# Held columns of one output remade on 16 engines' partitions and stored from GpSimd's queue

## The chip, the cores and the metric

The kernel runs on one core of one Trainium2 chip. The metric is the device time of one launch in microseconds (us). The profile gives the span from the first to the last instruction of one execution; the device time of that same execution is somewhat longer.

## The reference

For each of 8 x 12 = 96 heads the kernel multiplies a matrix x by the transpose of a matrix y:

```python
# x, y: [8, 12, 512, 64] float32
np.einsum('bhtc,bhsc->bhts', x, y).astype(np.float32)   # [8, 12, 512, 512]
```

It reads 25.17 MB and writes 100.66 MB.

## The kernel before

**Tiling.** Sixteen heads make a group, so there are 6 groups (`NG`). One load brings 128 partitions of 16 KB of x or y for one group (2 MB). A group has two halves, 12 in all (`NH`), and each half gives 4 outputs (`V`), 48 in all. An output `o` is a tile of 128 partitions of 4096 float32 (2 MB): partition p holds row p // 2 of one of two blocks, by p % 2.

**Stages.** `load` issues the loads from SyncE; the first five are issued inside a `tile_critical` section (line 367), the others as buffers come free. `compress` turns a loaded tile into bf16 (ScalarE, VectorE and GpSimd share it), `mix` rearranges x, and `transposes` makes `xT` and `yT` on VectorE. `all_products` is TensorE's loop: for each output, twice four matmuls of 128x512 into one of two PSUM tensors of four banks (`pms`). `result` copies each PSUM tensor into an output buffer (a slot of `pairs`), on ScalarE, for the very last output on VectorE. `store` issues the output's DMA from SyncE; from output 8 on two outputs go out in one DMA of 4 MB.

**Order and synchronisation.** The order of each engine's instructions is written out by hand. `emit` issues an instruction with the semaphore waits that its reads and writes need, as `need` works them out. A DMA signals a semaphore of its slot (`dma0` and so on), a DMA from GpSimd `dmapool`.

**Output 44** (`SHARED`) is stored in pieces, by `shares`. The 64 even partitions go in one DMA of 1 MB from SyncE. The 64 odd ones are divided, for each half b of 32 partitions: GpSimd issues three DMAs (10 rows, 6 rows, 16 rows), of which the first stores only the columns below N - HELD = 1024; SyncE then stores the columns above for 8 of these 10 rows. Two rows for each b, partitions 17 and 19 above 32b, are left without their last 3072 columns: these are the held columns.

**The held columns** are computed a second time at the end. `again` (line 288) runs 20 small matmuls with up to 16 columns of `xT` as weights, so that quarter c of the held columns comes to lie in the four partitions from 4c on, of which two are wanted. `rest` (line 305) copies the 16 partitions to the buffer `xk0` on VectorE and issues two DMAs from SyncE, one for each b, after the store of outputs 46 and 47 in the same queue. They signal `dma2` (`LAST`), as that store does.

**The end.** GpSimd waits for all semaphores but `dmapool` and `dma2`, clears those, and then waits for and clears the two late ones, one after the other (lines 405 to 415).

Of the kernel before, what the change touches and what calls it, by code (L numbers as in the profile page):

```python
# [9 lines left out]
def kernel(  # L10
# [3 lines left out]
    y: bass.AP,  # L14
    out: bass.AP,
):

# [4 lines left out]
    nc = tc.nc  # L24
    B, H, T, C = x.shape
    _, _, S, _ = y.shape
    P = 128
# [5 lines left out]
    V = G // 4  # L33
    K = 8
# [3 lines left out]
    N = K * S  # L38
    SINGLE = 2 * V
    SHARED = V * NH - V  # L40
    LAST = (V * NH - SINGLE - 2) // 2 % 3 * 2
    HELD = 6 * S
    fp32 = mybir.dt.float32
    bf16 = mybir.dt.bfloat16
    u32 = mybir.dt.uint32
# [9 lines left out]
    def buffer(name, width, dtype):  # L55
        return nc.alloc_sbuf_tensor(name, [P, width], dtype)[:, :]
# [4 lines left out]
    xks = [  # L61
        extra[:, :N // 2].bitcast(bf16) if i == 1 else buffer(f"xk{i}", R * C, bf16)
        for i in range(NG - 1)
    ]
# [9 lines left out]
    xTs = [buffer(f"xT{i}", K * D * E, u32) for i in range(2)]  # L74
    yTs = [buffer(f"yT{i}", D * R // 2, u32) for i in range(2)]
    pms = [nc.alloc_psum_tensor(f"pm{i}", [P, 4, S], fp32)[:, :, :] for i in range(2)]
    engines = {"act": nc.scalar, "dve": nc.vector, "pool": nc.gpsimd, "pe": nc.tensor, "sp": nc.sync}
    sems, ticks, snaps, writer, readers = {}, {}, {}, {}, {}
    known, own = {e: {} for e in engines}, {e: {} for e in engines}

    def need(name, points, told=True):

        best = {}
        for p, v in points:
            if known[name].get(p, 0) < v:
                best[p] = max(best.get(p, 0), v)
        for p, v in list(best.items()):
            if any(snaps[q, w].get(p, 0) >= v for q, w in best.items() if q != p):
                del best[p]
        for p, v in best.items():  # L90
            if told:
                engines[name].wait_ge(sems[p], v)  # L92
            known[name][p] = v
            for q, w in snaps[p, v].items():
                known[name][q] = max(known[name].get(q, 0), w)

    def promise(name, reads, writes):

        points = [writer[r] for r in (*reads, *writes) if r in writer]
        points += [v for w in writes for v in readers.get(w, ())]  # L100
        if name == "pool" and name in ticks:
            points.append((name, ticks[name]))
        return points

    def record(name, p, step, reads, writes, queue=False):
        at = (p, ticks.get(p, 0) + step)
        ticks[p] = at[1]
        if not queue:
            own[name][p] = at[1]
        snaps[at] = {**known[name], **own[name], p: at[1]}  # L110
        for r in reads:
            readers.setdefault(r, []).append(at)
        for w in writes:
            writer[w], readers[w] = at, []

    def signal(p):
        if p not in sems:
            sems[p] = nc.alloc_semaphore(p)
        return sems[p]

    def emit(name, make, reads=(), writes=(), dma=None, by=None, step=1):
        need(name, promise(name, reads, writes))
        p = by or name
        if dma is not None:
            p, step = f"dma{dma}", 16
        make().then_inc(signal(p), step)
        record(name, p, step, reads, writes, dma is not None)

    loaded = {}

    places = [0, 1, 2, 3, 4, 0, 1, 2, 3, 4, 1, 3]
    alone = [0, 2, 4, 0, 1, 3, 2, 4]
    heads = [0, 2, 1, 3]
# [3 lines left out]
    def copy(name, dst, src, reads, writes, by=None):  # L137
        emit(
            name,
            lambda: nc.scalar.activation(dst, src, COPY)  # L140
            if name == "act"
            else engines[name].tensor_copy(dst, src),  # L142
            reads,
            writes,
            by=by,
        )

    def both(*ids):
        return [("slot", i, pm) for i in ids for pm in range(2)]

    def place(ap, pattern):
        name = ap.tensor.name
        return mybir.PhysicalAccessPattern(
            ap=pattern, offset=ap.offset, dtype=ap.dtype, memref=name, memsetref=f"{name}_set"
        )

    def transfer(name, dst, src, to=None, of=None):

        to = to or dst.ap
        of = of or [src.ap[0], *[[1, 1]] * (len(to) - len(src.ap)), *src.ap[1:]]  # L160
        return engines[name].add_instruction(  # L161
            mybir.InstDMACopy(
                name=nc.get_next_instruction_name(),
                engine=engines[name].engine,
                ins=[place(src, of)],
                outs=[place(dst, to)],
                mode="Copy",
                cce_op=mybir.AluOpType.bypass,
                queue={"sp": "qSPDynamicHW", "pool": "qPoolDynamic"}[name],
            )  # L170
        )
# [82 lines left out]
    def all_products():  # L254
# [3 lines left out]
        with nc.Fori(1, V * NH + 1, 2 * V, engines=[nc.tensor.engine]) as first:  # L258
            for half in range(2):
                for j, h in enumerate(heads):  # L260
# [3 lines left out]
                    for p in range(2):  # L264
                        nc.tensor.wait_ge(sems[f"free{p}"], first + at)
                        products(half, h, 4 * p).then_inc(signal("pe"), 1)

    def shares(o, s):

        to, mine = ov[o // V, heads[o % V]], slots[s]  # L270
        line, w = to.ap[0][0], N - HELD

        def part(name, p, n, k, lo=0, hi=N):

            dst, src = to[p // 2:p // 2 + n, p % 2, lo:hi], mine[p:p + 2 * n - 1:2, lo:hi]
            emit(
                name, lambda: transfer(name, dst, src, [[line * n // k, k], [line, n // k], [1, hi - lo]]),
                reads=both(s), dma="pool" if name == "pool" else s,
            )

        for b in range(2):
            for p, n, k, hi in ((1, 10, 5, w), (21, 6, 3, N), (65, 16, 8, N)):
                part("pool", 32 * b + p, n, k, 0, hi)
        emit("sp", lambda: transfer("sp", to[:, 0], mine[::2]), reads=both(s), dma=s)
        for b in range(2):
            part("sp", 32 * b + 1, 8, 4, w)

    def again():

        half, h, part = SHARED // V % 2, heads[SHARED % V], HELD // 4  # L290
        xT = xTs[half].bitcast(bf16).rearrange("p (k h m) -> p k h m", k=K, h=V)
        yT = yTs[half].bitcast(bf16)
        for c in range(3, -1, -1):
            begin, end = N - HELD + c * part, N - HELD + (c + 1) * part
            cuts = sorted({begin, end, *range(begin, end, S), *(n for n in range(0, N, S) if begin < n < end)})
            for lo, hi in zip(cuts, cuts[1:]):
                for b in range(2):
                    last = nc.tensor.matmul(  # L298
                        pms[0][:4 * c + 4, 2 * b + (lo - begin) // S, (lo - begin) % S:(lo - begin) % S + hi - lo],
                        xT[:, lo // S, h, 32 * b + 16 - 4 * c:32 * b + 20],  # L300
                        yT[:, h * S + lo % S:h * S + lo % S + hi - lo], start=True, stop=True,
                    )
        return last

    def rest():

        half, part = SHARED // V % 2, HELD // 4
        to = ov[SHARED // V, heads[SHARED % V]]
        mine = xks[0][:16].bitcast(fp32)[:, :2 * part].rearrange("p (b s) -> p b s", b=2)
        emit("pe", again, [("xT", half), ("yT", half)], [("pm", 0)])  # L310
        copy(
            "dve", mine, pms[0][:16].rearrange("p (b j) s -> p b (j s)", b=2)[:, :, :part],
            [("pm", 0)], [("xk", 0)],
        )
        for b in range(2):
            dst, src = to[16 * b + 8:16 * b + 10, 1, N - HELD:], mine[1::2, b]
            emit(
                "sp", lambda: transfer(
                    "sp", dst, src, [[part, 4], dst.ap[0], [1, part]], [src.ap[0], [1, 1], src.ap[-1]]
                ),  # L320
                reads=[("xk", 0)], dma=LAST,
            )

    def store(o):
# [39 lines left out]
            for part in range(4):  # L364
                mix(i + 1, "dve", part)

    with tc.tile_critical():  # L367
        for n in range(SLOTS):
            load(n)
    tc.close()  # L370
# [26 lines left out]
    for o in range(V, V * NH):  # L397
        result(o)
        if o % V == V - 1:
            prepare(o // V + 2)  # L400
    all_products()
    rest()
    emit("sp", nc.sync.nop)

    last = f"dma{LAST}"
    late = ["dmapool", last]
    others = [p for p in sems if p not in late]
    need("pool", [(p, ticks[p]) for p in others])
    numbers = sorted(sems[p].num for p in others)
    runs = [n for n in numbers if n - 1 not in numbers]  # L410
    for n in runs:
        nc.gpsimd.sem_clear(range(n, next(m for m in range(n, n + len(sems) + 1) if m not in numbers)))
    for p in late:
        need("pool", [(p, ticks[p])])
        nc.gpsimd.sem_clear(sems[p])


# [28 lines left out]
```

## Time and profile before

| what | before |
|---|---|
| median of 3 runs | 297.98 us (297.93 to 298.37) |
| the profiled execution | 297.92 us |
| its span | 296.1 us |
| DMA traffic | 125.85 MB, 425 GB/s over the span |
| SyncE's queue | 5888 packets, 125.03 MB |
| GpSimd's queue | 288 packets, 0.80 MB |
| busy share of the span: PE, DVE, ACT, POOL | 47%, 53%, 70%, 20% |
| remade matmuls (line 298) | 20, 3.3 us |
| copy of the held columns on VectorE | 16 partitions x 1536, 1.7 us |
| stores of the held columns | 2 from SyncE, 24 KB each |

In the profile's lines PE is TensorE, DVE VectorE, ACT ScalarE, POOL GpSimd and SP SyncE; a q behind a name means the engine's sequencer. q1 is the DMA queue that SyncE's DMAs go through and q0 the one of GpSimd's. A group is shown as engine, line, operation, output<-input, number, busy time. The DMA row has one digit for each fortieth of the span: the busy share of the 16 DMA engines in tenths.

### The profile page before, as it was taken

The page shows a single profiled execution, that of the slowest core. Times are in us where ns is not written, and L with a number is a line of the kernel's source. Part 1 is how long each engine was busy: PE and PEld are TensorE (multiplying, and loading weights), DVE is VectorE, ACT ScalarE, POOL GpSimd, SP SyncE. Part 2 cuts the span into 40 slices and gives each one's busy share as a digit, 9 for nine tenths or more (in the row PEclk, how much of TensorE's full clock was granted, in tenths as well). Part 3 has the DMA queues.
Part 4 walks back from the last instruction along what each step waited for, and adds up shares of the span by engine and source line. Part 5 has one row for each costly group of instructions (what it writes and reads, how often), then busy time and mean ns, then how long its engine had stood idle before and what let it go on. Part 6 is the DMA issues. An engine that isn't in the chain of part 4 may idle for free.

```text
span 296.1 us, 1231 instructions
## 1 busy us (share of the span) xinstructions
PE 139.9 (47%) x404; PEld 37.9 (13%) x404; DVE 158.0 (53%) x76; ACT 208.2 (70%) x107; POOL 59.5 (20%) x29
## 2 busy tenths in 40 slices
PE   0000040437576557556654655577546646575400
PEld 0000010112111111111111111111111111121200
DVE  2167798899929594925808529258095240002600
ACT  1664666999999999666966696669666976684000
POOL 2399999992000000000000000000000000040000
PEclk9999995657779997778789776765798787756855
DMA  7999999999999999999999999999999999999998
GB/s 272 427 429 427 432 429 427 432 425 425 427 438 427 460 425 426 425 429 447 429 456 426 425 429 425 425 438 434 434 456 425 425 429 429 425 438 422 415 436 348
DMA packets 6178, 125.85 MB, mean 425 GB/s; under 512 B 896, under 2 KB 896, under 8 KB 932
## 3 DMA queue, kind: packets, MB, share of 16 engines
q1 hardware_dynamic: 5888, 125.03, 98.7%
q0 software_dynamic: 288, 0.80, 0.7%
q14 instruction: 2, 0.02, 0.0%
HBM read 25.17 MB, written 100.66 MB: 425 GB/s over the span
## 4 chain that ended last, share of the span: by engine, by line
DMA 56%; ACT 23%; PE 7%; issue 4%; DVE 3%; SPq 0%; ACTq 0%
DMA out_dram<-pair 43%; ACT pair L140 21%; DMA pair<-in_y_dram 7%; DMA pair<-in_x_dram 6%; PE pm L248 6%; DVE pair L142 3%; ACT xk L140 1%; PE pm L298 1%; ACT yb L140 1%; DVE xk L142 1%; SPq L177 0%; ACTq L92 0%; SPq L371 0%; SPq L367 0%
## 5 line engine op out<-in xcount | busy, mean ns | idle before, releaser
L248 PE MATMUL pm<-yT,xT 128*128 128x512 bf16 x384 | 136.6, 501 | 137.3 <-ACT pair L140 100.0
L140 ACT ACTIVATE pair<-pm 128x2048 f32<-128x2048 f32 x94 | 170.6, 1883 | 41.3 <-DMA out_dram<-pair 37.5
L225 DVE STREAM_TRANSPOSE xT<-xb 128x2048 uint32<-128x2048 uint32 x12 | 46.7, 3893 | 69.1 <-PE pm L248 66.7
L248 PEld LDWEIGHTS pm<-yT,xT 128*128 128x128 bf16 x384 | 36.0, 115 | 237.0 <-ACT pair L140 156.0
L161 POOL DMA_DIRECT2D out_dram<-pair x6 | 3.5, 583 | 193.7 <-ACT pair L140 193.7
L142 DVE COPY xb<-xk 32x2048 bf16<-32x2048 bf16 x32 | 41.7, 1304 | 0.9
L142 DVE CAST yb<-pair 64x2048 bf16<-64x2048 f32 x10 | 30.7, 3074 | 9.5 <-DMA pair<-in_y_dram 9.3
L140 ACT ACTIVATE xk<-pair 128x4096 bf16<-128x4096 f32 x5 | 18.1, 3617 | 10.4 <-DMA pair<-in_x_dram 10.3
L142 POOL COPY xb<-xk 32x2048 bf16<-32x2048 bf16 x8 | 23.5, 2939 | 6.7 <-ACT xk L140 6.2
L142 DVE COPY pair<-pm 128x2048 f32<-128x2048 f32 x2 | 4.5, 2286 | 31.9 <-PE pm L248 31.9
L234 DVE STREAM_TRANSPOSE yT<-yb 128x1024 uint32<-128x1024 uint32 x10 | 19.2, 1918 | 0.0
L140 ACT ACTIVATE yb<-pair 64x2048 bf16<-64x2048 f32 x5 | 12.4, 2472 | 3.9 <-DMA pair<-in_y_dram 3.8
L142 POOL CAST yb<-pair 64x2048 bf16<-64x2048 f32 x5 | 14.5, 2903 | 1.2 <-DMA pair<-in_y_dram 0.8
L142 POOL COPY xb<-pair 32x2048 bf16<-32x2048 bf16 x4 | 12.7, 3184 | 0.3
L140 ACT ACTIVATE pair<-pair 128x4096 bf16<-128x4096 f32 (+1 forms) x2 | 6.1, 3030 | 3.7 <-DMA pair<-in_x_dram 2.5
L142 DVE CAST pair<-pair 64x2048 bf16<-64x2048 f32 x2 | 5.4, 2694 | 4.0 <-DMA pair<-in_y_dram 4.0
L142 DVE COPY xb<-pair 32x2048 bf16<-32x2048 bf16 x4 | 5.2, 1306 | 0.1
L140 ACT ACT_TABLE_LOAD x1 | 1.3, 1283 | 4.4 <-PEq L371 4.4
L378 DVE MEMSET xb<- 128x2048 uint32 x1 | 1.8, 1765 | 4.9 <-PEq L371 4.9
L234 DVE STREAM_TRANSPOSE yT<-pair 128x1024 uint32<-128x1024 uint32 x2 | 3.9, 1946 | 0.0
L298 PE MATMUL pm<-yT,xT 128*16 128x256 bf16 (+5 forms) x20 | 3.3, 333 | 0.6 <-DVE pair L142 0.6
L142 POOL CAST pair<-pair 64x2048 bf16<-64x2048 f32 x1 | 3.3, 3293 | 0.1
(7 smaller groups left out, 5.8 us busy)
## 6 DMA issues: line engine op xcount, KB each, us to landing
out_dram<-pair SPq DMA_DIRECT2D x19, 4096.0 KB, 21.8
out_dram<-pair SPq DMA_DIRECT2D x9, 2048.0 KB, 9.3
pair<-in_x_dram SPq DMA_DIRECT2D x6, 2048.0 KB, 18.8
pair<-in_y_dram SPq DMA_DIRECT2D x6, 2048.0 KB, 16.5
out_dram<-pair SPq DMA_DIRECT2D x1, 1024.0 KB
out_dram<-pair POOLq DMA_DIRECT2D x2, 256.0 KB, 16.6
out_dram<-pair SPq DMA_DIRECT2D x2, 96.0 KB
out_dram<-pair POOLq DMA_DIRECT2D x2, 96.0 KB, 14.6
```

What stands on the lines that cost most here:

```text
L140: lambda: nc.scalar.activation(dst, src, COPY)
L142: else engines[name].tensor_copy(dst, src),
L161: return engines[name].add_instruction(mybir.InstDMACopy(name=nc.get_next_instruction_name(), engine=engines[name].engine, ins=[place(src, ...
L225: lambda: nc.vector.transpose(xTs[half].rearrange("p (k r e) -> p k e r", k=K, e=E), xbs[half].rearrange("p (k e c) -> p k e c", k=K, e=E),),
L234: lambda: nc.vector.transpose(yTs[half].rearrange("p (r j) -> p j r", r=D), ybs[half][b].rearrange("p (j c) -> p j c", c=D),),
L248: last = nc.tensor.matmul(pms[k // 4][:, j, :], xT[:, k + j, h, :], yT[:, h * S:(h + 1) * S], start=True, stop=True,)
L298: last = nc.tensor.matmul(pms[0][:4 * c + 4, 2 * b + (lo - begin) // S, (lo - begin) % S:(lo - begin) % S + hi - lo], xT[:, lo // S, h, 32 ...
L378: lambda: engines[name].memset(xbs[half], 0.0),
```

## The change

- 7 instead of 6 blocks of 512 columns are held (`HELD`), so 3584 columns. GpSimd's first DMA of each b stores 512 columns of its ten rows, and SyncE's DMAs 3584 columns of eight rows.
- `again` cuts the held columns into eighths of 448 columns. Eighth q of half b is remade in the partitions from 64b + 4q on. To place it there, the weights begin 64b + 4q columns of `xT` ahead of the wanted ones; what lies below is written over by the pieces that come later in the loop. There are 28 matmuls, all into one PSUM bank.
- `rest` copies 96 partitions of 448 columns on VectorE, and GpSimd instead of SyncE issues the stores: three DMAs, of 5, 3 and 8 eighths (`turns`), with two rows of 448 columns in each. They signal `dmapool`.
- `shares` takes its division of the odd rows from the same `turns`; rows and engines are as before.
- The semaphores of `late` are allocated first, so that each set of semaphores is one range: GpSimd waits for the early ones and clears them at once, then waits for both late ones and clears them at once.
- The section with the first five loads is synchronised by ScalarE in place of SyncE, whose loads it holds.

```diff
-    HELD = 6 * S
+    HELD = 7 * S
...
+    turns = [(0, 5), (5, 3), (8, 8)]
...
+    late = [f"dma{LAST}", "dmapool"]
+    for p in late:
+        signal(p)
...
+    def part(name, dst, src, k, reads, dma):
+        assert src.ap[0][1] == 2 * k and dst.ap[0][1] == k
+        emit(
+            name, lambda: transfer(name, dst, src, dst.ap),
+            reads=reads, dma=dma,
+        )
...
     def shares(o, s):
...
+        def odd(name, b, e, k, lo, hi):
+            p = 4 * e + 32 * b + (32 if e > 7 else 0)
+            n = 2 * k
+            dst = to[p // 2:p // 2 + n, 1, lo:hi].rearrange("(k i) n -> k i n", i=2)
+            part(name, dst, mine[p + 1:p + 2 * n:2, lo:hi], k, both(s), "pool" if name == "pool" else s)
         for b in range(2):
-            for p, n, k, hi in ((1, 10, 5, w), (21, 6, 3, N), (65, 16, 8, N)):
-                part("pool", 32 * b + p, n, k, 0, hi)
+            for e, k in turns:
+                odd("pool", b, e, k, 0, N if e else w)
         emit("sp", lambda: transfer("sp", to[:, 0], mine[::2]), reads=both(s), dma=s)
         for b in range(2):
-            part("sp", 32 * b + 1, 8, 4, w)
+            odd("sp", b, 0, 4, w, N)
...
     def again():
...
+        for b in (1, 0):
+            for q in range(7, -1, -1):
+                begin, end = N - HELD + q * width, N - HELD + (q + 1) * width
+                cuts = [begin, *(n for n in range(0, N, S) if begin < n < end), end]
+                for lo, hi in zip(cuts, cuts[1:]):
+                    stop = (lo // S * V + h) * P + 32 * b + 20
                     last = nc.tensor.matmul(
+                        pms[0][:64 * b + 4 * q + 4, 0, lo - begin:hi - begin],
+                        xT[:, stop - 64 * b - 4 * q - 4:stop],
...
     def rest():
...
+        mine = xks[0][:64 + 32].bitcast(fp32)[:, :width]
         emit("pe", again, [("xT", half), ("yT", half)], [("pm", 0)])
+        copy("dve", mine, pms[0][:64 + 32, 0, :width], [("pm", 0)], [("xk", 0)])
+        for e, k in turns:
+            b, q = divmod(e, 8)
+            dst = to[16 * b + 8:16 * b + 10, 1, N - HELD + q * width:N - HELD + (q + k) * width]
+            p = 64 * b + 4 * q
+            part(
+                "pool", dst.rearrange("i (k n) -> k i n", n=width), mine[p + 1:p + 4 * k:2],
+                k, [("xk", 0)], "pool",
             )
...
-    with tc.tile_critical():
+    with tc.tile_critical(sync_engine=nc.scalar.engine):
...
+    for points in ([p for p in sems if p not in late], late):
+        need("pool", [(p, ticks[p]) for p in points])
+        numbers = [sems[p].num for p in points]
+        assert max(numbers) - min(numbers) == len(points) - 1
+        nc.gpsimd.sem_clear(range(min(numbers), max(numbers) + 1))
```

## The prediction

> **What bounds the kernel now.** I read the page's slices and queue table first, then the packets of the last microseconds, because the change touches only the first microsecond and the last thirty.
>
> The page, span, slices and DMA queues (packets, MB, share of 16 engines):
>
> ```profile
> span 296.1 us, 1231 instructions
> ...
> DMA  7999999999999999999999999999999999999998
> ...
> q1 hardware_dynamic: 5888, 125.03, 98.7%
> q0 software_dynamic: 288, 0.80, 0.7%
> ```
>
> The 16 DMA engines are busy in every slice. In the trace's packet records (start, time, size, queue of each) the first packets start at 1.99 to 2.46 us, and from there the packets of one engine follow each other without a gap. So the end is the first start plus the longest engine's own sum of packet times; work of PE, DVE, ACT or POOL counts only if a store is issued too late, or if it makes packets slower. The question is which engine ends last, and by how much.
>
> The DMA view of 295 to 295.7 us:
>
> ```profile
> DMA packets 34, 0.05 MB, mean 70 GB/s; under 512 B 18, under 2 KB 18, under 8 KB 34
> ...
> q1 hardware_dynamic: 34, 0.05, 18.7%
> ```
>
> These are the held columns: 16 packets of 3072 B (the two stores of `rest`, 24 KB each) and small 4 B completion writes. They take 0.121 us each and run on only four engines, four in a row on each, behind the last 32 KB packets of the store of outputs 46 and 47. By the packet records the 16 engines end their last 32 KB packet between 294.62 and 295.33 us, the four at 295.01, 295.06, 295.17 and 295.20; these four go on to 295.49 to 295.68. The last completion lands 0.34 us later, at 296.02; GpSimd's last semaphore clear ends the span at 296.09. The profiled execution took 297.92 us, so 1.83 us lie outside the span; it stands 0.06 us below the median, 297.98.
>
> How the held columns come about, in the chain of waits (start, us, what), and SyncE's and GpSimd's timelines:
>
> ```profile
> 272.21 2.30 DVE pair L142
> 274.51 0.04 issue
> 274.56 3.35 PE pm L298 x20
> 277.91 0.02 issue
> 277.93 1.75 DVE xk L142
> ```
>
> ```profile
> 276.73 0.58 SPq L161 DMA_DIRECT2D out_dram<-pair  x1
> 279.70 2.00 SPq L161 DMA_DIRECT2D out_dram<-xk  x2
> ```
>
> ```profile
> 262.35 3.48 POOL L161 DMA_DIRECT2D out_dram<-pair  x6 [193.71 <-ACT pair L140]
> ```
>
> The held stores are issued by 281.7, 13 us before their packets run: the chain ahead of them is not on the path. How GpSimd's queue is served, in the DMA view of 267.5 to 284 us:
>
> ```profile
> q1 hardware_dynamic: 320, 6.11, 87.0%
> q0 software_dynamic: 288, 0.80, 12.2%
> ```
>
> All 288 packets of the six GpSimd stores lie in this stretch: 18 per engine, 4 of data and 14 of 4 B, so 9 for each turn of three stores (5, 3 and 8 engines). On each engine they alternate with SyncE's packets one for one. The first starts at 267.6, 4.6 us after its issue ended (263.05), which is about four 1.215 us packets of SyncE's queue.
>
> **The change part by part.** *1. The held stores leave SyncE's queue.* Removed from four engines: 4 x 0.121 us and two completion writes of 0.009, 0.50 us at the very end of each. These four then end at 295.01 to 295.20.
>
> *2. They go to GpSimd's queue, over 16 engines.* Two rows of 448 columns per engine, 2 packets of 1792 B. From the rows 3072 B at 0.121 and 4096 B at 0.159 us the slope is 0.037 ns per byte, so about 0.073 us each. With the 7 small packets of a turn (0.009 us each, by the six stores before) it is 2 x 0.073 + 7 x 0.009 = 0.21 us more on every engine. The four end at 295.4; of the twelve others the last goes from 295.33 to 295.54.
>
> *3. 7 instead of 6 blocks of columns are held.* This concerns rows 17, 19, 49 and 51 of output 44, whose engine I call the fifth. It carried 48 KB less than its equals; now 56 KB less. By 32 KB in 1.215 us that is 0.30 us less; with part 2 it ends 0.09 us earlier than before. It isn't the last in my reading: the packets of the engine that ends at 295.33 carry a full share of GpSimd's 16 KB rows. If it were, the new last would be the next, 295.29 + 0.21 = 295.50, no great difference. Engines 0 to 3 swap 2 KB per row between queues, at equal bytes.
>
> *4. Three more stores prepared by GpSimd slow SyncE's packets.* While GpSimd issued its six (262.35 to 265.83), 32 KB packets begun at 264 to 266 averaged 1.232 us and those begun at 266 to 268 1.256, against 1.215 in the microseconds before 260. Summed over the packets that is 0.107 us per engine, at most 0.38 on one. Half as many stores: 0.05, at most 0.19. While the queues alternate they stay at 1.220 against 1.217 late in the tail: 0.03 more. I take 0.08 together, nearer to the mean than to the worst engine because the last engine needn't be the worst hit; bounds 0 and 0.25.
>
> The Trainium skill, "DMA: Bandwidth & Descriptors", in "Latency and other measured facts", says that two of the engines, 7 and 15, are usually slower, and guesses at contention with the descriptor rings of GpSimd's path. By it the whole disturbance, 16 x 0.05 = 0.86 us with unrounded values, would fall on two engines, 0.43 us each as an estimate, and the time would be 0.35 us over my sum, about 298.3. The trace speaks against so sharp a split, with at least ten engines showing packets over 1.235 us there.
>
> *5. PE, DVE and the issues.* The remake has 28 matmuls instead of 20 and 7168 streamed columns instead of 6144. Late in the group a 256-column matmul takes 0.108 us, so 1024 more columns cost 0.43, and about 0.3 more goes to the four 64-column ones and eight more weight loads of 0.09 to 0.14 (which mostly overlap): PE ends near 278.7 instead of 277.9. DVE's copy is 96 partitions of 448 instead of 16 of 1536; its cost goes by columns (1536 in 1.745, 2048 in 2.286, so 1.06 ns per column and 0.12 fixed): 0.6 instead of 1.75 us. The data is ready at about 279.6, as before (279.68). GpSimd issues three stores at 0.56 to 0.70 us each, until about 281.4. What is queued behind its wait are only the final waits and clears; SyncE ends earlier, with nothing behind. Cover: the queue's earlier packets end at 283.7 on the engines with 16 KB rows, and the nine new rounds follow, three at SyncE's 16 KB pace (0.62) and six at 1.22, so they are done near 293, some 2 us before SyncE's queue is. All this costs nothing then; without that cover, see the second rival.
>
> *6. The end.* Now both late semaphores are waited for ahead of one clear. If one wait becomes an instruction of its own behind the last landing it costs about 0.06 us (a 0.017 us instruction and the gap to the next, as in the first microsecond's rows); if not, nothing, since the merged clears lie in 286.1 to 286.5. I take 0.03.
>
> *7. The first section.* SyncE leaves the start barrier at 0.67 us, runs a NOP at 0.72 and a branch that waits on it at 0.80, and issues its first load at 0.96. With ScalarE doing the NOP, SyncE saves an instruction slot of 0.08 us but waits for another engine's semaphore, which took about 0.03 us from GpSimd's release to SyncE's start at 0.65. I take 0.03 gained; bounds 0.10 gained and 0.10 lost. It passes whole to the end, as nothing idles on the DMA engines. The section's exit only moves work that starts at 4.4 and whose first load lands at 8.7.
>
> The sum: the last packet moves from 295.68 to 295.54 + 0.08 = 295.62, -0.06; the end +0.03; the start -0.03. That is -0.06 us: 297.92 becomes 297.86, and against the median 297.98 it is 297.92. I say 297.9.
>
> **The rivals.** *Faster: the four engines were the whole excess.* If the order among the twelve others differs from execution to execution, they may end near the mean of the 16 (295.0), and the new end is 295.0 + 0.21 = 295.2; with the best ends for the start (-0.10) and no disturbance that is -0.58, and a first packet that is also less slow (the first 16 KB packets took 1.04 to 2.10 us against 0.611 in steady state, so a few tenths are there) brings it over 0.6: about 297.2. For it: the excess of the four is plain, 0.35 us over the next. Against: the three times before agree within 0.15%, which speaks for a fixed order.
>
> *Slower: GpSimd's queue becomes the last.* If its new packets begin not right behind the old ones but 4.6 us and more after the last issue (286 and later), nine rounds at 1.22 us end at 297. By my reading the rest of a queue runs at 0.009 us a packet once SyncE's is empty, which caps the loss at about 0.2. It decides if such leftovers don't run back to back, for instance because their descriptors are fetched one turn at a time: then the end is 297.0 + 0.4 instead of 296.09, and the time 299.2. The point is a first held packet later than 285 us on any engine. For it: landings of GpSimd's stores took 12.4 to 16.6 us, and 281.4 + 14 is 295.4. Against: those figures contain six stores in one line and rounds slowed by 16 KB rows.
>
> *The change doesn't reach its engines.* If GpSimd's shares didn't fall on 5, 3 and 8 consecutive engines, two packets would move from one to another, 0.15 us: 298.0, inside the forecast.
>
> **How the numbers follow.** A difference of about 0.2%, 0.6 us, is what a measurement of this kernel can tell from no change. No change as worked out: 0.54, own range 297.5 to 298.3 (disturbance 0 to 0.25, start, the spread of the times before). Faster rival: 0.26. Slower rival: 0.20, of which most lies between the capped 298.2 and 299.2. The range that leaves out 2 in 10 is 297.2 to 298.9.
>
> **What would show it.** Right: queue q0 with 432 packets, no 3072 B packets, the last packets of the span 32 KB ones that end within 0.2 us of 295.6, held packets done by 294, 28 matmuls near 4.1 us, a DVE copy near 0.6, the first load issued between 0.86 and 1.06. Wrong: packets of q0 behind the last 32 KB packet for more than 0.2 us; 32 KB packets above 1.23 us around 280 to 284; or a first packet that starts more than 0.1 us away from 1.99.

## The result and the profile after

The changed kernel takes 299.03 us (median of 8 runs, 298.85 to 299.20) against 297.99 for the kernel before (8 runs, 297.88 to 298.40). The ratio is 1.0033 with a 95% interval of 1.0024 to 1.0042: 1.0 us slower, where I had forecast no change at 297.9 and a range of 297.2 to 298.9.

The changed kernel's page, span and DMA queues (packets, MB, share of 16 engines):

```profile
span 297.1 us, 1248 instructions
...
q1 hardware_dynamic: 5864, 125.01, 98.4%
q0 software_dynamic: 352, 0.82, 0.7%
q8 instruction: 1, 0.02, 0.0%
q14 instruction: 2, 0.02, 0.0%
```

The same table of the kernel before:

```profile
q1 hardware_dynamic: 5888, 125.03, 98.7%
q0 software_dynamic: 288, 0.80, 0.7%
q14 instruction: 2, 0.02, 0.0%
```

The row to see is q8: one packet of kind instruction, 16,384 bytes, on a queue that the kernel before didn't use. The two of q14 were there before. The DMA view of 278 to 282 us places it:

```profile
DMA packets 190, 1.67 MB, mean 418 GB/s; under 512 B 86, under 2 KB 86, under 8 KB 86
...
q1 hardware_dynamic: 106, 1.31, 78.9%
q0 software_dynamic: 83, 0.34, 21.1%
q8 instruction: 1, 0.02, 1.5%
```

And the DMA view of 295.4 to 296.7 us, the end:

```profile
DMA packets 4, 0.03 MB, mean 25 GB/s; under 512 B 3, under 2 KB 3, under 8 KB 3
...
q1 hardware_dynamic: 4, 0.03, 6.0%
```

A share of 6.0% is one engine of sixteen. One single 32 KB packet starts after 295.4; three others are completion writes. In the packet records fifteen engines end their last 32 KB packet between 294.95 and 295.58 us, as forecast, and one ends at 296.64. That engine is the one with the q8 packet. (The records name no engine. A packet is taken to follow the one whose end meets its start, and some of these links have more than one candidate.) Followed back, it ran three 16 KB packets of 0.912, 0.904 and 0.978 us around q8's own 0.929, where its neighbours' took about 0.61. So it lost 0.93 + 0.30 + 0.29 + 0.37 = 1.89 us, and would have ended near 294.75 without them. 0.8 us of the loss fits into this engine's slack; 1.07 us, 296.64 against the next engine's 295.58, goes into the time.

The held columns themselves were ready in time. Timeline of the changed kernel around the remake:

```profile
274.51 5.65 PE L313 MATMUL pm<-yT,xT 128*96 128x448 bf16 x28 [0.61 <-DVE pair L149]
...
280.20 0.62 DVE L149 COPY xk<-pm 96x448 f32<-96x448 f32 x1 [3.54 <-PE pm L313]
281.12 1.70 POOL L168 DMA_DIRECT2D out_dram<-xk  x3 [15.34 <-DVE xk L149]
```

The data was ready at 280.8 and the last packet of q0 ended at 293.15 us, ahead of the last packets of q1. The 16 packets of held columns started between 285.27 and 291.46 us.

### The profile page after: what moved, and what is told of

It is laid out like the page before. It is cut to its first block, busy times and chain, and to the rows that moved or that the text cites. A ratio compares the mean times of both kernels' runs of the same rounds, so it can differ in the third digit from the quotient of the medians.

```text
span 297.1 us, 1248 instructions
## 1 busy us (share of the span) xinstructions
PE 142.7 (48%) x412; PEld 39.3 (13%) x412; DVE 156.8 (53%) x76; ACT 208.2 (70%) x107; POOL 61.2 (21%) x32
## 4 chain that ended last, share of the span: by engine, by line
DMA 61%; ACT 23%; PE 4%; issue 4%; DVE 2%; SPq 0%; ACTq 0%
DMA out_dram<-pair 47%; ACT pair L147 21%; DMA pair<-in_y_dram 7%; DMA pair<-in_x_dram 6%; PE pm L255 4%; DVE pair L149 2%; ACT xk L147 1%; ACT yb L147 1%; SPq L184 0%; ACTq L95 0%; SPq L383 0%; ACTq L379 0%
## 5 line engine op out<-in xcount | busy, mean ns | idle before, releaser
L313 PE MATMUL pm<-yT,xT 128*96 128x448 bf16 (+27 forms) x28 | 5.7, 386 | 0.6 <-DVE pair L149 0.6
L168 POOL DMA_DIRECT2D out_dram<-xk x3 | 1.7, 569 | 15.3 <-DVE xk L149 15.3
```

The lines of the kernel that those rows point to most:

```text
L168: return engines[name].add_instruction(mybir.InstDMACopy(name=nc.get_next_instruction_name(), engine=engines[name].engine, ins=[place(src, ...
L313: last = nc.tensor.matmul(pms[0][:64 * b + 4 * q + 4, 0, lo - begin:hi - begin], xT[:, stop - 64 * b - 4 * q - 4:stop], yT[:, h * S + lo % ...
```

## Experiments

**Whose instructions?** Three engines have a longer program after the change: TensorE has eight more matmuls (each a weight load and a matmul, so 16 instructions), ScalarE takes part in the first section, GpSimd issues three more DMAs. SyncE's program became shorter. Two edits undo one part of the change, two make one part alone.

`a_sp_section`, the changed kernel with the section given back to SyncE:

```diff
-    with tc.tile_critical(sync_engine=nc.scalar.engine):
+    with tc.tile_critical():
```

> The changed kernel with its first section synchronised by SyncE again. Three theories of the one 16 KB packet of kind instruction (queue q8) that the changed kernel has at 279.4 us, and of its 1.0 us. T1, TensorE: eight more remade matmuls (16 instructions) make TensorE's program so long that one more block of it is fetched late: the q8 packet stays, about 299.0 us. T2, ScalarE: the section gives ScalarE four instructions more, and it is ScalarE's block: no q8 packet, about 298.0 us. T3, the fetch is beside the point and GpSimd's held stores cost the time: about 299.0 us, q8 as it may be. Of the section itself I expect the first load issued near 0.96 instead of 0.92 us, 0.04 us later.

298.95 us against 298.06 for the kernel before, ratio 1.003 (1.0019 to 1.004), with the q8 packet at 279.39 us. The first load was issued at 0.963 us. ScalarE's part isn't the cause.

`b_act_section`, the reverse edit in the kernel before:

> The kernel before with only the section's synchronisation given to ScalarE. T1 (TensorE's program) and T3 (GpSimd's stores): no q8 packet, within 0.1 us of the kernel before, first load at 0.92 us. T2 (ScalarE's four more instructions): a q8 packet near the end and about 1 us more, 299.0 us.

298.06 against 298.06, ratio 1.0 (0.9991 to 1.001), no q8 packet. The first load is issued at 0.926 instead of 0.963 us and the first packet starts 0.03 us earlier; no measured time shows it. T2 is refuted from both sides.

`b_more_mm`, the kernel before with eight more small matmuls behind the remake:

```diff
+        for _ in range(8):
+            last = nc.tensor.matmul(
+                pms[0][:4, 3, 0:64], xT[:, N // S - 1, h, 32 + 16:32 + 20],
+                yT[:, h * S + S // 2:h * S + S // 2 + 64], start=True, stop=True,
+            )
         return last
```

> The kernel before with eight more small matmuls (64 columns, into an unused part of a PSUM bank) at the end of the remake: 28 instead of 20, nothing else changed. T1: a q8 packet of 16 KB near 279 us on one DMA engine and 0.5 to 1.5 us more than before, about 299.0 us. T2 and T3: no q8 packet, no difference, since the held columns are ready 13 us before their stores run.

298.83 against 298.06, ratio 1.0027 (1.0017 to 1.0036). Its page has the row of the changed kernel, with SyncE's and GpSimd's queues exactly as before the change:

```profile
q1 hardware_dynamic: 5888, 125.03, 98.4%
q0 software_dynamic: 288, 0.80, 0.7%
q8 instruction: 1, 0.02, 0.0%
```

The packet runs at 279.44 us for 0.931 us. One engine ends at 296.53, the others, with their held packets, by 295.91. None of the other edits is in this kernel.

`a_20mm`, the changed kernel with eight matmuls fewer; it leaves out the narrower pieces, so a part of the held columns isn't remade:

```diff
+                pieces = list(zip(cuts, cuts[1:]))
+                if 1 < q < 6:
+                    pieces = [max(pieces, key=lambda c: c[1] - c[0])]
-                for lo, hi in zip(cuts, cuts[1:]):
+                for lo, hi in pieces:
```

> The changed kernel with 20 instead of 28 remade matmuls: of the pieces of each of the four middle eighths only the wider one is computed, so a part of the held columns keeps old values. T1: no q8 packet, about 297.9 us, the time that I had forecast. T2 and T3: as the changed kernel, 299.0 us.

297.86 against 298.06, ratio 0.9992 (0.9982 to 1.0001), and its page lists no q8:

```profile
q1 hardware_dynamic: 5864, 125.01, 98.6%
q0 software_dynamic: 352, 0.82, 0.7%
q14 instruction: 2, 0.02, 0.0%
```

Queues, copy, stores and section are those of the changed kernel. With 20 matmuls the loss is gone, so T3 falls as well.

**The work or the length?** `b_nops16` is the kernel before with 16 TensorE instructions that compute nothing, behind the remake:

```diff
     rest()
+    for _ in range(16):
+        emit("pe", nc.tensor.nop, by="pad")
```

> The kernel before with 16 instructions on TensorE behind the remake that compute nothing (each only counts up a semaphore of its own): the program is as long as with the eight more matmuls. If the program's length causes the fetch: a q8 packet of 16 KB and about 298.9 us, as with eight more matmuls. If the matmuls themselves do (their work or the later data): no q8 packet and 298.0 us.

298.85 against 298.00, ratio 1.0031 (1.0019 to 1.0043); its page:

```profile
span 296.9 us, 1247 instructions
...
q8 instruction: 1, 0.02, 0.0%
```

No matmul was added, and the held stores are issued by 281.8 us (281.7 before). The length of TensorE's program is enough. Here the packet runs at 282.37 us, 0.929 us, and one engine ends at 296.42, the others by 295.63.

**Where the boundary lies.** `b_more4`, `b_more2` and `b_more1` have `range(4)`, `range(2)` and `range(1)` in the loop of `b_more_mm`. Each has one measured time.

> The kernel before with four more small matmuls, 8 TensorE instructions, half of what brought the q8 packet. It halves the interval in which the boundary lies: a q8 packet (and about 298.9 us) if it lies within the first eight instructions, none (and 298.0 us) if behind them.

298.69 us, with the q8 packet at 282.30.

> The kernel before with two more small matmuls, 4 TensorE instructions. Eight more brought the fetch, none more did not. A q8 packet and about 298.7 us if the boundary lies within the first four, none and 298.0 us if behind them.

298.12 us, without it, beside 298.28 for the kernel before on the same chip.

> The kernel before with one more small matmul, 2 TensorE instructions: a q8 packet and about 298.7 us only if the program before ends right at the boundary. I expect none and 298.0 us.

298.13 us, without it. So with four more TensorE instructions the packet isn't there, and with eight it is. The single times alone wouldn't tell, as one of 23 of the kernel before was 298.67; but in `b_more4` one engine again ends last, at 296.35, and the others by 295.80. `b_more2`'s page against `b_more4`'s, each the span and the instruction queues (in `b_more2`'s count six records of matmuls are missing):

```profile
span 296.3 us, 1229 instructions
...
q14 instruction: 2, 0.02, 0.0%
```

```profile
span 296.9 us, 1239 instructions
...
q8 instruction: 1, 0.02, 0.0%
q14 instruction: 2, 0.02, 0.0%
```

**The queue alone.** `b_pool_queue` is the kernel before with its two held stores on GpSimd's queue:

```diff
-                "sp", lambda: transfer(
-                    "sp", dst, src, [[part, 4], dst.ap[0], [1, part]], [src.ap[0], [1, 1], src.ap[-1]]
+                "pool", lambda: transfer(
+                    "pool", dst, src, [[part, 4], dst.ap[0], [1, part]], [src.ap[0], [1, 1], src.ap[-1]]
...
-                reads=[("xk", 0)], dma=LAST,
+                reads=[("xk", 0)], dma="pool",
```

> The kernel before with its two held stores issued by GpSimd instead of SyncE, all else as before (20 matmuls, four engines for each store). By my sum: the 3072 B packets run ahead of the last 32 KB packets instead of behind them, the last packet ends near 295.4 to 295.6 instead of 295.68, 0.1 to 0.3 us faster than before. If GpSimd's queue is served too late (the rival by which I had priced the slower case): packets of q0 behind 295.4 us and 0.5 us or more slower.

298.10 against 298.00, ratio 1.0005 (0.9996 to 1.0014). The first half of the expectation held: the packets of q0 end at 290.83 us and the last packet is a 32 KB one. The gain didn't come: the last packet ends at 295.70. Eight engines now end between 295.38 and 295.70, the eight others between 294.61 and 295.05, and 32 KB packets begun at 287 to 290 us average 1.250 us (1.218 before), one of them 1.480. The held rows run as eight packets of 6144 B. Followed back in the same way, these lie on engines that end late, and none lies on the eight early ones. Taking the packets from the end of four engines and giving them to eight is worth nothing.

**A shorter remake that is complete.** `a_seven` cuts the held columns into seven pieces of 512 columns for each half, so that no piece crosses a block of `yT`: 14 matmuls. The stores have 5, 2 and 7 pieces.

```diff
-        half, h, width = SHARED // V % 2, heads[SHARED % V], HELD // 8
+        half, h, width = SHARED // V % 2, heads[SHARED % V], S
...
-            for q in range(7, -1, -1):
+            for q in range(HELD // S - 1, -1, -1):
...
-        half, width = SHARED // V % 2, HELD // 8
+        half, width = SHARED // V % 2, S
...
-        for e, k in turns:
+        for e, k in ((0, 5), (5, 2), (8, 7)):
```

> The changed kernel with its held columns cut into seven pieces of 512 instead of eight of 448 for each half: the cuts fall on the blocks of 512, so 14 remade matmuls instead of 28, on 14 partition groups. If the longer TensorE program is the whole loss: no q8 packet, 297.8 to 297.9 us, that is 0.1 to 0.2 us under the kernel before and 1.1 under the changed one. If GpSimd's stores cost something too: 298.1 or more.

297.83 against 298.00, ratio 0.9997 (0.9988 to 1.0006): 1.2 us under the changed kernel's 299.03, and not to be told from the kernel before. Its page and its timeline:

```profile
span 295.9 us, 1220 instructions
...
q14 instruction: 2, 0.02, 0.0%
```

```profile
274.49 3.32 PE L313 MATMUL pm<-yT,xT 128*92 128x512 bf16 x14 [0.48 <-DVE pair L149]
```

No q8 packet; the 16 engines end between 294.87 and 295.47 us. What the other edits bring is then at most this: a last packet 0.2 us earlier than before in the profiled run, and no difference clear of noise in the time.

## Why the prediction was wrong

**The step that failed is part 5.** It took the eight more matmuls as TensorE time, found cover for it (GpSimd's queue done near 293, some 2 us ahead of SyncE's), and wrote "All this costs nothing then". The cover was real: in the changed kernel GpSimd's queue was done at 293.15 us, 3.5 us ahead of the end. What added instructions can also cost, by making the program longer, was not in the sum at all. The 16 KB that bring the next stretch of the program run through the same 16 DMA engines, of which none has an idle moment, and all of it lands on one of them: 1.89 us of one engine in the changed kernel, 1.07 us of them beyond the next. The before profile showed the kind of traffic: two packets of 8 KB in its q14 row, at 116 and 161 us, 0.309 us each. I had read past them as small.

**No rival had it.** The slower rival was wrong in its mechanism. The point that I had named for it was met: every held packet started after 285 us, the first at 285.27. But q0 was done at 293.15 us and no packet of q0 lay behind the last 32 KB packets, so this lateness cost nothing. That the time landed between the forecast and that rival's 299.2 is chance.

**The rest of the sum is not contradicted by `a_20mm`,** which has all of the change but the longer program. Its interval, 0.9982 to 1.0001, holds the forecast of 0.06 us less, but also no change at all. By parts:

- Parts 1 and 2: no 3072 B packet is left at the end, and the last packet ends at 295.60 us; I had 295.62, or 295.59 with the start's 0.03. The two rows of 1792 B come as one packet of 3584 B (16 of them, 0.140 us each), 0.146 us by my rows. There are 352 packets in q0 and not 432, since small ones are merged too.
- Part 3: one engine ends at 295.60, the next at 295.36. Whether that engine is the fifth, or the one that ended last of the twelve before, was not followed, so the close figure of parts 1 and 2 may be luck.
- Part 4: against the kernel before, the later packets of q1 cost 0.07 us more per engine (16 KB ones after 276 us 0.622 against 0.618, 32 KB ones at 284 to 293 us 1.233, 1.222 and 1.218 against 1.223, 1.218 and 1.217 in steps of 3 us). I had taken 0.08.
- Part 5's sizes: the copy took 0.62 us (0.6). The 28 matmuls took 3.4 us in `a_sp_section` and 5.7 in the changed kernel's profiled run (I had 4.1); between 275 and 280 us the granted clock was 1.00 in the first and 0.57 in the second (0.93 before), which I had not allowed for. It made no difference, as said there: both runs have the q8 packet and the same loss. GpSimd's packets were done at 288.9 us in `a_20mm`, earlier than my 293.
- Part 6: from the end of the last packet to the start of the last clear 0.48 us instead of 0.37, 0.11 us where I took 0.03; in `a_seven` it is 0.40.
- Part 7: 0.037 us, where I took 0.03.

The sum gave 297.86 us for the profiled execution and 297.92 for the median; `a_20mm` measured 297.95 and 297.86. The 0.09 us by which the profiled execution is longer are mostly part 6.

**What was known and could have told it.** The Trainium skill, "Runtime: NRT & Kernel Launch", section "Instruction fetch mechanics", says that an engine's program is refilled in blocks of 16 KiB, 256 instructions, through a DMA queue of its own, and that crossing a block boundary costs "one DMA tail-bump, mostly hidden". The block size and the separate queue agree with this trace (16,384 bytes, q8); the two packets of kind instruction on q14 have 8,192 bytes. "Mostly hidden" doesn't agree: in this kernel, whose DMA engines have no idle time to hide it, it cost 0.7 to 1.2 us: 299.03 against 297.86 with and without eight matmuls of the changed kernel, 298.83 against 298.06, 298.85 against 298.00 and, in one execution, 298.69 against 298.00 with and without instructions added to the kernel before.

**Still open:** when TensorE asks for the block (the packet runs at 279.4 us in the three kernels with eight more matmuls and at 282.3 with 16 empty instructions or four matmuls), how many instructions of the launch itself count towards the boundary, and which of the 16 engines carries it. That a block ends between the fourth and the eighth added instruction is inferred; the runs show only that the packet comes with eight and not with four.

## What to carry to other kernels

In a kernel that keeps all DMA engines busy, count the instructions that a change adds to each engine's program, not only their time: here TensorE's program could grow by four instructions for nothing and by eight at the price of about 0.7 us (one execution each). Look at the instruction rows of the DMA queue table, before and after: a new one is the first thing to follow up, as it was here. And a cut of the columns that falls on the blocks of `yT` (14 matmuls instead of 28) can save more than the matmuls' time, by the instructions that it saves.

## What the runs showed of the hardware

The q8 packet costs its DMA engine twice its own time. In each of the five kernels that have it, this packet of 0.93 us stands between three 16 KB packets, two ahead of it and one behind, that took 0.84 to 1.01 us instead of 0.61: 0.912, 0.904 and 0.978 in the changed kernel, 0.875, 0.928 and 1.006 in `b_nops16`, whose q8 packet came 3 us later. Summed up, the engine lost 1.89 to 1.91 us each time. Why the neighbours are slower isn't shown.

GpSimd's and SyncE's packets alternated one for one on each engine while both queues had work (in the kernel before, 447 of the 456 handovers between 269 and 281 us that could be matched). In GpSimd's stores two short rows were merged into one packet (2 x 1792 B in the changed kernel, 2 x 3072 B in `b_pool_queue`). That saves little: 0.140 us for 2 x 1792 B, against 0.146 by my rows for two packets.
